# A hybrid diffusion layer on one core: the first tile's modulation in two halves, its shift used with the fifth tile, and the squares of the last four tiles in two calls

## The chip, the core and the metric

The kernel runs on one core of a Trainium2 chip. The time is that of one execution on the device in microseconds. Before the change it was 1232.01 us, the median of 3 runs (1231.84 to 1232.99).

Names used below: PE is the engine for matrix products (its weight loads are PEld), DVE the vector engine, ACT the engine for functions and copies, POOL the general engine, SP the engine that issues loads. Each engine works through its own queue in order and waits on counters of the others.

## The reference, cut to what matters

The layer works on 512 latent tokens and 256 context tokens of 1024 channels. The stage that the change touches is the first one:

```
mod = silu(c) @ w_mod + b_mod            # shift sh1 and scale sc1 are its first two parts
h_lat = rmsnorm(x, norm1_g) * (1 + sc1) + sh1
h_ctx = rmsnorm(ctx, norm1_g) * (1 + csc1) + csh1     # the same weights, from c_ctx
p_lat = h_lat @ w_in                     # its columns: z, xBC, dt, q, k, v, gates
```

All later work (two token mixers, their merge, and the gated feed-forward part) follows from `h_lat` and `h_ctx` and is the same in both kernels.

## The kernel before

Channels lie on the 128 partitions, so `x` is eight tiles of 128 channels by 512 tokens (`xs_`, printed as `xsb`). Products in float32 are made of three: a value is split into a high and a low part, and high by high, low by high and high by low are added.

The opening stage computes the modulation and, in the same stretch, the first five of sixteen gate column blocks (`w0`, 640 columns) into five PSUM banks `pg` (printed as `mis`). Its steps are named by a letter and a tile number j:

- **A**j (`mod_rows`): 8 matmuls of `silu(c)` with the two 512 KB pieces of `wm1` that hold the shift and scale columns of tile j, into columns 0 to 255 of the PSUM tile `pmod` (printed as `acc`); the first 4 need the first piece, the last 4 the second. Then ACT copies the row out (`tm`), and the 640 columns of `w0` are split (`w0h`, `w0l`).
- **B**j (`mod_cols`): two small matmuls turn the row into columns 256 to 259 of the same `pmod`; ACT makes of them the factor `a1` (first) and the shift `s1` (then; it is part of `s32`).
- **H**j (`prep`): for j below 4 (`NU`) the raw tile times `a1`, split into `ah` (ACT) and `al` (DVE), because the token norms are not known yet; for j from 4 on the normalised and shifted tile (`norm`: DVE makes the product, ACT `hlh`, DVE `hll`). **N**j is the same for the first four tiles, later.
- **P**j:ab (`products`): the three products of tile j into the banks a to b-1.
- **Z**j (`shifts`): the shift of tile j times `w0`, into `pbias`, since the first four tiles went in without their shift.
- **sq** (`squares`): ACT squares a tile, DVE adds it to `ssq`. **sum_l** (PE), a root on DVE and POOL, and **put_l** (PE) spread the token norms; ACT copies them to `r_l`; **scale_a/b** multiply the five banks by them on DVE.
- **hold**, **keep**: matmuls whose result nobody reads.

After the eight tiles follows the first of the large products (`gemm` of q), in whose middle the context's sum (`sum_c`, from `te`) and its spreading are done.

PE's order is fixed by the string `order` (the schedule is manual for PE). The queues of DVE, ACT and POOL are ordered by the framework's scheduler from the same calls, so they move when the calls move. SP issues loads in the order of the calls; it has eight completion counters in turn, so a load is issued only after the load eight places ahead of it has landed, and also when its buffer is free: `wm` has 6 buffers, `w0` has 4. A PSUM tile counts as one thing for these waits: a matmul into one part of `pmod` waits for the copies out of any other part that stand ahead of it in the calls.

Of the kernel before, what the change touches and what calls it, by code (L numbers as in the profile page):

```python
# [9 lines left out]
F32 = mybir.dt.float32  # L10
F32R = mybir.dt.float32r
U8 = mybir.dt.uint8
AF = mybir.ActivationFunctionType
# [5 lines left out]
P = 128  # L19
D = 1024  # L20
L = 512
LC = 256
KT = D // P
# [4 lines left out]
V_BMOD = 0  # L28
V_N1 = 48
# [15 lines left out]
def tile_hybrid_layer(  # L45
# [33 lines left out]
    V, S, G, T = nc.vector, nc.scalar, nc.gpsimd, nc.tensor  # L79
# [221 lines left out]
    NU, NG = 4, 5  # L301
    first = {}
    gates = []
    with tc.tile_pool(name="spool", bufs=1) as sp:
# [10 lines left out]
        def load_mod(i):  # L315
            t = sp.tile([P, 4, 256], F32, tag="wm", name="wm", bufs=6)
            nc.sync.dma_start(t, wm1[i].rearrange("p (k c) -> p k c", k=4))
            return t

        def load_w0(j):  # L320
            r = sp.tile([P, 640], F32, tag="w0", name="w0", bufs=4)
            nc.sync.dma_start(r, w0[j])
            return r

        def load_x(k):
            nc.sync.dma_start(xs_[:, 2 * k : 2 * k + 2, :], xT[k].rearrange("p (k t) -> p k t", k=2))
# [2 lines left out]
            nc.sync.dma_start(xs_[:, k, :], xT[k // 2, :, k % 2 * L : k % 2 * L + L])  # L329

        nc.sync.dma_start(ccs, cc)
        mod_raw = {i: load_mod(i) for i in range(2)}
        nc.sync.dma_start(ident, ident_d)
        nc.sync.dma_start(vec[:, :V_N2], vecs[:, :V_N2])
        w0_raw = {0: load_w0(0)}
# [4 lines left out]
        mod_raw.update({i: load_mod(i) for i in (4, 5)})  # L340
        w0_raw[2] = load_w0(2)
        load_x(1)
        load_x(2)
        load_x(3)
        mod_raw.update({i: load_mod(i) for i in (6, 7)})
        w0_raw[3] = load_w0(3)
        nc.sync.dma_start(vec[:, V_N2:], vecs[:, V_N2:])
        G.memset(raw(still), 1.0)
        G.memset(csil32, 0.0)
# [17 lines left out]
        def mod_rows(j):  # L367

            for u in range(2):
                i = 2 * j + u  # L370
                w = mod_raw.pop(i) if i in mod_raw else load_mod(i)
                for k in range(4):
                    z = slice(32 * k, 32 * k + 32)
                    T.matmul(pmod[z, 0:256], csil32[:, 4 * u + k, :], w[:, k, :], start=u == 0, stop=u == 1)
            row = tmp("tm")[:, :256]
            tc.keep_in_program_order(S.copy(row, pmod[:, 0:256]))
            if j + 1 < KT and j + 1 not in w0_raw:
                w0_raw[j + 1] = load_w0(j + 1)
            W[j] = split_w(j)
            return row  # L380

        def mod_cols(j, row):
            for i in range(2):
# [10 lines left out]
        def squares(x_, q, n, ks):  # L394
            for k in ks:
                sq = tmp(("ta", "tb")[k % 2])[:, :n] if k else q
                tc.keep_in_program_order(S.activation(sq, x_[:, k, :], AF.Square))
                if k:
                    V.tensor_tensor(q, q, sq, ALU.add)
# [17 lines left out]
        def products(j, w, h, gs=range(NG)):  # L417

            st, en = j == 0, j in (NU - 1, KT - 1)
            for a, b in ((0, 0), (0, 1), (1, 0)):  # L420
                for i in gs:
                    T.matmul(  # L422
                        pg[i], w[a][:, i * P : (i + 1) * P], h[b], start=st and a + b == 0, stop=en and a == 1,
                        skip_group_check=True,
                    )

        def shifts(j):

            for g in range(3):
                n = 256 if g < 2 else P  # L430
                T.matmul(
                    pbias[32 * g : 32 * g + 32, 0:n], s32[:, j, :], w0_raw[j][:, 256 * g : 256 * g + n],
                    start=j == 0, stop=j == NU - 1,
                )

        r, W, H = {}, {}, {}
# [16 lines left out]
        def hold(n):  # L453
            for _ in range(n):
                T.matmul(unread[:, :256], still[:, :P], still, start=True, stop=True)
# [21 lines left out]
        def load_next():  # L477
# [18 lines left out]
            "sq_0": lambda: squares(xs_, ssq, L, range(1)),  # L496
            "sq_1": lambda: squares(xs_, ssq, L, range(1, 2)),
            "sq_2": lambda: squares(xs_, ssq, L, range(2, 4)),
            "sq_3": lambda: squares(xs_, ssq, L, range(4, 8)),
            "hold": lambda: hold(18),  # L500
            "keep": lambda: hold(6),
            "sq_c": lambda: squares(xc_, cq, LC, range(4)),
            "sq_d": lambda: squares(xc_, cq, LC, range(4, 8)),
            "sum_l": lambda: sums("l", ssq, 4),
# [11 lines left out]


        order = """
            hold A0 keep B0 H0 sq_0 keep Z0 P0:02 A1 P0:23 B1 H1 sq_1 P0:35 A2 P1:02 B2 H2 sq_2 P1:25 Z1 P2:02 sq_3 A3 P2:23 B3 H3
            P2:35 sum_l Z2 P3:02 A4 put_l P3:23 B4 H4 P3:35 scale_a Z3 scale_b rows A5 half P4:02 B5 H5 cols P4:25 A6  # L520
            P5:02 B6 H6 P5:24 A7 ctx N0 P5:45 B7 H7 next P6:02 N1 P6:25 N2 P7:02 sq_c N3 P7:25 sq_d
        """
        with tc.manual_schedule(engines={mybir.EngineType.PE}):
# [1563 lines left out]
def pack(  # L2087
    x, c, ctx, c_ctx, w_mod, b_mod, norm1_g, norm2_g, w_in, ssd_conv_w, ssd_conv_b, ssd_dt_bias, ssd_a_log, ssd_d,
    ssd_norm_g, w_o_ssd, w_o_att, att_sink, w_out, w_up, ffn_conv_w, ffn_conv_b, w_down, final_g,
):  # L2090
    f = lambda a: np.asarray(a)
    x, c, ctx, c_ctx, w_mod, w_in = f(x), f(c), f(ctx), f(c_ctx), f(w_mod)[0], f(w_in)[0]
    w_o_ssd, w_o_att, w_out, w_up, w_down = f(w_o_ssd)[0], f(w_o_att)[0], f(w_out)[0], f(w_up)[0], f(w_down)[0]
    ca = np.ascontiguousarray
    z0, xbc0, dt0 = 0, 2048, 5120
    q0 = dt0 + 64
    k0, v0, g0 = q0 + 1024, q0 + 1280, q0 + 1536
    half = np.r_[0:16, 32:48, 16:32, 48:64]
    perm = lambda base, heads: np.concatenate([base + 64 * h + half for h in range(heads)])
    A = np.arange  # L2100
    d = {}
    d["xT"] = ca(x[0].T.reshape(4, 2, P, L).transpose(0, 2, 1, 3).reshape(4, P, 2 * L))
    d["ctxT"] = ca(ctx[0].T.reshape(2, 4, P, LC).transpose(0, 2, 1, 3).reshape(2, P, 4 * LC))
    d["cc"] = ca(np.stack([c[0], c_ctx], 1).reshape(KT, P, 2).transpose(1, 0, 2))
    cw, fw = f(ssd_conv_w)[0], f(ffn_conv_w)[0]
    d["vecs"] = ca(
        np.concatenate(
            [_per_channel(f(a)) for a in (b_mod[0], norm1_g[0], norm2_g[0], final_g, ssd_norm_g[0])]
            + [_per_channel(cw[i]) for i in range(3)]
            + [_per_channel(f(ssd_conv_b)[0])]  # L2110
            + [_per_channel(fw[i]) for i in range(3)]
            + [_per_channel(f(ffn_conv_b)[0])],
            axis=1,
        )
    )
    dta = np.stack([f(ssd_dt_bias)[0].reshape(64), f(ssd_a_log)[0].reshape(64)], 1).reshape(2, 1, 32, 2)
    d["dta"] = ca(np.repeat(dta, 2, axis=1).reshape(P, 2))
    d["bc"] = ca(np.concatenate([f(ssd_d)[0], f(att_sink)[0]]))
    d["wm1"] = ca(w_mod[:, :2048].reshape(2, 4, P, 2, KT, P).transpose(4, 0, 2, 1, 3, 5).reshape(16, P, 1024))
    d["wm2"] = ca(w_mod[:, 2048:].reshape(4, 2, P, 8, 512).transpose(3, 0, 2, 1, 4).reshape(8, 4, P, 1024))  # L2120
    d["wq"] = _cols(w_in, perm(q0, 16))
    d["wk"] = _cols(w_in, perm(k0, 4))
    vdt = ca(w_in[:, np.r_[v0:g0, dt0:q0]].reshape(KT, P, 320).transpose(1, 0, 2)).reshape(P, KT * 320)
    d["wv"] = ca(np.pad(vdt, ((0, 0), (0, 320))).reshape(P, 3, 960).transpose(1, 0, 2))
    d["w0"] = ca(w_in[:, g0 : g0 + 640].reshape(KT, P, 640))
    d["wx"] = _cols(w_in, A(xbc0, dt0))
    d["wz"] = _cols(w_in, A(z0, xbc0))
    d["wg"] = _cols(w_in, A(g0, g0 + 2048))
    d["woa"] = _cols(w_o_att, A(1024))
    d["wos"] = _cols(w_o_ssd, A(1024))  # L2130
    d["wout"] = _cols(w_out, A(1024))
    d["wup"] = _cols(w_up, A(2 * NFF * P))
    wd = np.pad(w_down.reshape(11, 2, P, 2, 512), ((0, 1), (0, 0), (0, 0), (0, 0), (0, 0)))
    d["wdn"] = ca(wd.reshape(6, 2, 2, P, 2, 512).transpose(2, 4, 0, 3, 1, 5).reshape(4, 6, P, 1024))
    d["ident_d"] = np.eye(P, dtype=np.float32)
    inv = (10000.0 ** (-np.arange(0, 32, 2, dtype=np.float32) / np.float32(32))).astype(np.float32)
    t = np.arange(L)
    ang = np.concatenate([(t // 64).astype(np.float32)[None] * inv[:, None], (t % 64).astype(np.float32)[None] * inv[:, None]])
    cos, sin = np.cos(ang).astype(np.float32), np.sin(ang).astype(np.float32)
    d["cos_d"] = ca(np.tile(cos, (4, 1)))  # L2140
    d["sin_d"] = ca(np.tile(np.concatenate([-sin, sin]), (2, 1)))
    qq, kk = np.arange(P)[:, None], np.arange(384)[None]
    win = np.where((kk >= qq) & (kk <= qq + 256), 0.0, -NEG).astype(np.float32)
    zero = np.zeros((P, 256), np.float32)
    d["win_d"] = np.concatenate([zero, win, zero], axis=1)
    d["sel_d"] = (np.arange(P)[:, None] > np.arange(P)[None]).astype(np.float32)
    d["bm"] = ca(f(b_mod)[0, 5120:6144].reshape(2, 512))
    d["fg"] = ca(f(final_g))
    return d
# [12 lines left out]
```

## Time and profile before

| | |
|---|---|
| time, median of 3 runs | 1232.01 us |
| the profiled execution, its own time | 1232.22 us |
| its span in the trace | 1230.4 us (1.8 us lie outside it) |
| ACT busy | 687.0 us (56%) |
| DVE busy | 914.1 us (74%) |
| POOL busy | 167.9 us (14%) |
| bytes moved | 224.65 MB, mean 183 GB/s |
| granted PE clock | 0.998 of full speed |

In the first 60 us the queue of SP moves 17.91 MB. "Busy" counts an instruction from start to end; the matmuls of PE overlap each other, and their ends are modelled. A row of a timeline gives the start, the duration, engine, line, operation, what it writes and reads, how many there are, and in brackets how long its engine was idle ahead of it and what ended that. One float32 matmul of the program stands as two in the trace. The chain of waits gives for each piece the time by which it moved the end.

### The profile page before, as it was taken

The numbers are of one execution on the slowest core, as the hardware profiler recorded it, in microseconds if no ns is written. First come the engines' busy times: TensorE is split into PE (matmuls) and PEld (weight loads), VectorE is DVE, ScalarE is ACT, GpSimd is POOL, SyncE is SP. The second block draws the span as 40 slices with busy tenths as digits, with TensorE's granted clock in tenths as the row PEclk, the third lists the DMA queues.
The fourth block names the chain that finished last, engine by engine and source line by source line (L and its number), as shares of the span: only waits on it lengthen the run. The fifth ranks groups of instructions, "written<-read, shape, count | busy, mean of one in ns | idle before, by whom it ended". The sixth has DMA issues, their size and how long they took to land.

```text
span 1230.4 us, 17460 instructions
## 1 busy us (share of the span) xinstructions
PE 1218.5 (99%) x6328; PEld 996.3 (81%) x6328; DVE 914.1 (74%) x1484; ACT 687.0 (56%) x1302; POOL 167.9 (14%) x174
## 2 busy tenths in 40 slices
PE   9999999999999999999999999999999999999997
PEld 6798888888878877777777778888988888888886
DVE  4757888888555698697886786677688788886566
ACT  4657787787443556566586572223544444444543
POOL 0000111121100033333351530000200000000000
PEclk9999999999999999999999999999999999999999
DMA  9652678877946235345347466776144444457785
GB/s 354 245 159 89 218 194 194 212 198 211 225 141 211 91 123 147 121 131 185 122 138 203 136 205 221 225 245 236 48 166 148 145 150 153 153 169 248 243 318 183
DMA packets 108630, 224.65 MB, mean 183 GB/s; under 512 B 9600, under 2 KB 48832, under 8 KB 108544
## 3 DMA queue, kind: packets, MB, share of 16 engines
q1 hardware_dynamic: 101056, 197.32, 48.9%
q0 software_dynamic: 6912, 25.17, 8.7%
q8 instruction: 50, 0.82, 0.3%
q10 hardware_dynamic: 576, 1.05, 0.2%
q14 instruction: 36, 0.29, 0.1%
HBM read 193.29 MB, written 49.87 MB: 198 GB/s over the span
## 4 chain that ended last, share of the span: by engine, by line
PE 92%; DVE 3%; DMA 2%; ACT 2%; issue 1%; SPq 0%; POOLq 0%; ACTq 0%; DVEq 0%
PE acc L197 19%; PE acc L200 19%; PE acc L198 19%; PE acc L1919 3%; PE acc L1917 3%; PE acc L1918 3%; PE score L811 3%; PE po L860 3%; PE pt L847 2%; PE mis L1480 2%; PE mis L1385 2%; DMA wm<-wm 1%; PE mis L422 1%; PE acc L930 1%; PE acc L931 1%; PE acc L932 1%
## 5 line engine op out<-in xcount | busy, mean ns | idle before, releaser
L197 PE MATMUL acc<-hlh,whi 128*128 128x512 f32 x488 | 199.3, 408 | 0.0
L150 DVE TENSOR_TENSOR wlo<-wraw,whi 128x1024 fp32r<-128x1024 f32 (+2 forms) x119 | 143.4, 1207 | 71.9 <-ACT whi L149 62.2
L149 ACT CAST whi<-wraw 128x1024 fp32r<-128x1024 f32 (+2 forms) x119 | 122.8, 1033 | 127.4 <-PE acc L198 75.0
L200 PE MATMUL acc<-hlh,wlo 128*128 128x512 f32 x488 | 191.4, 392 | 0.0
L198 PE MATMUL acc<-hll,whi 128*128 128x512 f32 x488 | 190.7, 391 | 0.0
L197 PE MATMUL acc<-mh,whi 128*128 128x512 f32 x360 | 141.0, 392 | 0.0
L200 PE MATMUL acc<-mh,wlo 128*128 128x512 f32 x360 | 140.1, 389 | 0.0
L198 PE MATMUL acc<-ml,whi 128*128 128x512 f32 x360 | 140.0, 389 | 0.0
L200 PEld LDWEIGHTS acc<-hlh,wlo 128*128 128x128 f32 x488 | 91.6, 188 | 20.3
L198 PEld LDWEIGHTS acc<-hll,whi 128*128 128x128 f32 x488 | 91.9, 188 | 17.5 <-issue 1.7
L197 PEld LDWEIGHTS acc<-hlh,whi 128*128 128x128 f32 x488 | 91.8, 188 | 17.5 <-issue 2.2
L198 PEld LDWEIGHTS acc<-ml,whi 128*128 128x128 f32 x360 | 67.6, 188 | 14.5 <-issue 0.5
L197 PEld LDWEIGHTS acc<-mh,whi 128*128 128x128 f32 x360 | 67.6, 188 | 14.3 <-issue 0.5
L200 PEld LDWEIGHTS acc<-mh,wlo 128*128 128x128 f32 x360 | 67.6, 188 | 14.2
L820 DVE CUSTOM_DVE_ANT_0 p<-score,winm,nsink 128x512 f32<-128x512 f32 (+1 forms) x64 | 51.9, 810 | 15.2 <-PE score L811 13.7
L1268 DVE SCALAR_TENSOR_TENSOR ta<-acc,half,ta 128x511 f32<-128x511 f32 (+1 forms) x66 | 43.8, 663 | 25.7 <-ACT ta L1267 25.6
L1267 ACT ACTIVATE ta<-acc,half 128x512 f32<-128x512 f32 (+1 forms) x66 | 46.7, 708 | 27.0 <-PE acc L200 25.7
L1275 ACT ACTIVATE tb<-ta 128x512 f32<-128x512 f32 (+1 forms) x44 | 23.5, 534 | 65.2 <-DVE ta L1269 59.2
L827 ACT ACTIVATE p<-p,mneg 128x512 f32<-128x512 f32 (+1 forms) x64 | 49.7, 777 | 15.3 <-DVE mneg L820 14.7
L1387 POOL TENSOR_TENSOR st<-st,eT 128x512 f32<-128x512 f32 x24 | 33.5, 1396 | 170.5 <-ACT st L1405 162.3
L197 PE MATMUL acc<-hch,whi 128*128 128x256 f32 x176 | 54.4, 309 | 0.0
L855 DVE TENSOR_TENSOR ptl<-pt,pth 128x512 fp32r<-128x512 f32 x72 | 47.5, 686 | 8.5 <-ACT pth L851 7.8
(503 smaller groups left out, 2970.1 us busy)
## 6 DMA issues: line engine op xcount, KB each, us to landing
wraw<-wup SPq DMA_DIRECT2D x44, 512.0 KB, 3.6
wt_d<-wdn POOLq DMA_DIRECT2D x36, 512.0 KB, 7.8
fb<-cs_d SPq DMA_DIRECT2D x32, 512.0 KB, 6.6
wraw<-wm SPq DMA_DIRECT2D x32, 512.0 KB, 4.1
wraw<-wx SPq DMA_DIRECT2D x24, 512.0 KB, 3.5
wraw<-wt_d SPq DMA_DIRECT2D x20, 512.0 KB, 4.0
sp_d<-te SPq DMA_DIRECT2D x33, 256.0 KB, 2.1
wm<-wm SPq DMA_DIRECT2D x16, 512.0 KB, 7.7
```

The costliest lines, as they stand in the source:

```text
L149: S.copy(hi[:, :n], r[:, :n])
L150: V.tensor_tensor(lo[:, :n], r[:, :n], raw(hi[:, :n]), ALU.subtract)
L197: T.matmul(ps, wh, xh[:, k0 + k, :], start=a, stop=False)
L198: T.matmul(ps, wh, xl[:, k0 + k, :], start=False, stop=False)
L200: T.matmul(ps, wl, xh[:, k0 + k, :], start=False, stop=b)
L811: T.matmul(ps[:, o : o + len(z) * P], Q[h][:, b * P : (b + 1) * P], k[:, j, z[0] * P : (z[-1] + 1) * P], start=v == 0 and o % 512 in (0, P ...
L820: V.tensor_tensor_reduce(p[:, :w], d["ps"][i][:, o0 : o0 + w], m, op0=ALU.add, op1=ALU.min, scale=1.0, scalar=nsink[:, h : h + 1], accum_o ...
L827: S.activation(p, p, AF.Exp, bias=d["mneg"][:, i : i + 1], scale=-1.0, accum_out=d["den"][:, i : i + 1])
L855: V.tensor_tensor(d["ptl"][x], d["pt"][x], raw(d["pth"][x]), ALU.subtract)
L860: T.matmul(d["po"], vst[:, cols[x], j, :], d[y][x], start=x == 0 and y == "pth", stop=x == c - 1 and y == "ptl")
L1267: S.activation(o[:, :n], ps[:, :n], AF.Identity, scale=hcol(base_w, stride + i), bias=hcol(base_b, i))
L1268: V.scalar_tensor_tensor(o[:, 1:n], ps[:, 0 : n - 1], hcol(base_w, i), o[:, 1:n], ALU.mult, ALU.add)
```

## The change

The first tile's two pieces of `wm1` are packed anew: piece 0 holds all scale columns of tile 0, piece 1 all its shift columns. Piece 0 is the first load; piece 1 goes behind all tiles of `x`. `A0` and `B0` are gone; `S0` and `a0` make the scale from piece 0 alone (8 matmuls of 128 columns, one small matmul, one activation), and `T0` and `s0` make the shift later, next to `A4` and `B4`, in other columns of the same `pmod`. `Z0` moves next to `Z3`, and the first `Z` to start `pbias` is now `Z1`. The pieces 6 and 7 of `wm1` and the `w0` of tile 3 are loaded ahead of the last four tiles of `x`, no longer behind them. The squares of tiles 4 to 7 are two calls, one ahead of tile 3's `H` and one behind it, and `sum_l` and `put_l` stand later. For tile 0 the product with `w0l` comes ahead of that with `al`. The twelve matmuls of the two `keep` become 3 and 8. `w0` has 7 buffers in place of 4.

```diff
-            r = sp.tile([P, 640], F32, tag="w0", name="w0", bufs=4)
+            r = sp.tile([P, 640], F32, tag="w0", name="w0", bufs=7)
...
-        mod_raw = {i: load_mod(i) for i in range(2)}
+        mod_raw = {0: load_mod(0)}
...
         load_x(1)
+        mod_raw.update({i: load_mod(i) for i in (6, 7)})
+        w0_raw[3] = load_w0(3)
         load_x(2)
         load_x(3)
-        mod_raw.update({i: load_mod(i) for i in (6, 7)})
-        w0_raw[3] = load_w0(3)
+        mod_raw[1] = load_mod(1)
         nc.sync.dma_start(vec[:, V_N2:], vecs[:, V_N2:])
...
+        def first_rows(i):
+            w = mod_raw.pop(i).rearrange("p k c -> p (k c)")
+            z0 = 0 if i == 0 else 3 * P
+            for u in range(2):
+                for k in range(4):
+                    z, c = slice(32 * k, 32 * k + 32), P * (4 * u + k)
+                    T.matmul(
+                        pmod[z, z0 : z0 + P], csil32[:, 4 * u + k, :], w[:, c : c + P], start=u == 0, stop=u == 1,
+                    )
+            row = tmp("tc")[:, :P]
+            tc.keep_in_program_order(S.copy(row, pmod[:, z0 : z0 + P]))
+            if i == 0:
+                W[0] = split_w(0)
+            return row
+
+        def first_cols(i, row):
+            c = 258 if i == 0 else 260
+            T.matmul(pmod[:, c : c + 2], row, sel2, start=True, stop=True)
+            if i == 0:
+                S.activation(a1[:, 0, :], pmod[:, c : c + 2], AF.Identity, scale=col(V_N1, 0), bias=bp1[:, 0:1])
+            else:
+                S.activation(s1[:, 0, :], pmod[:, c : c + 2], AF.Identity, bias=col(V_BMOD, 0))
...
-            for a, b in ((0, 0), (0, 1), (1, 0)):
+            for a, b in ((0, 0), (0, 1), (1, 0)) if j else ((0, 0), (1, 0), (0, 1)):
...
-                    start=j == 0, stop=j == NU - 1,
+                    start=j == 1, stop=j == NU - 1,
...
-            "sq_3": lambda: squares(xs_, ssq, L, range(4, 8)),
+            "sq_3": lambda: squares(xs_, ssq, L, range(4, 6)),
+            "sq_4": lambda: squares(xs_, ssq, L, range(6, 8)),
...
-            hold A0 keep B0 H0 sq_0 keep Z0 P0:02 A1 P0:23 B1 H1 sq_1 P0:35 A2 P1:02 B2 H2 sq_2 P1:25 Z1 P2:02 sq_3 A3 P2:23 B3 H3
-            P2:35 sum_l Z2 P3:02 A4 put_l P3:23 B4 H4 P3:35 scale_a Z3 scale_b rows A5 half P4:02 B5 H5 cols P4:25 A6
+            hold S0 keep_a a0 H0 sq_0 keep_b P0:02 A1 P0:23 B1 H1 sq_1 P0:35 A2 P1:02 B2 H2 sq_2 P1:25 Z1 P2:02 A3 sq_3 P2:23 B3 H3 sq_4
+            P2:35 Z2 P3:02 sum_l A4 T0 P3:23 B4 s0 put_l H4 P3:35 scale_a Z0 Z3 scale_b rows A5 half P4:02 B5 H5 cols P4:25 A6
...
+    for i in range(2):
+        d["wm1"][i] = wm[:, :, :, 1 - i, 0].transpose(2, 0, 1, 3).reshape(P, 1024)
```

Three places show what the engines' queues make of it. The first is PE's queue from the end of tile 2's products to A5, before. L241 is sum_l, L431 a Z, L422 products, L374 A4 and then A5, L258 put_l, L384 B4.

```order
L241 MATMUL acc<-rmsc,ssq 128x1 x4
L431 MATMUL acc<-w_143,s_117 32x256 x2
...
L374 MATMUL acc<-wm,csil_116 32x256 x8
L258 MATMUL acc<-ident,rs 128x128 x4
...
L384 MATMUL acc<-sel_119,tm 128x2 x2
...
L431 MATMUL acc<-w_152,s_117 32x256 x2
L431 MATMUL acc<-w_152,s_117 32x128
L374 MATMUL acc<-wm,csil_116 32x256 x8
```

The same stretch of PE's queue in the changed kernel, from the last product of tile 3's first two banks on. L375 is A4 (A5 in the last row), L390 is T0, L401 is s0, and L456 with `w_127` is Z0.

```order
L447 MATMUL mis<-ah,w0l 128x512 x2
L241 MATMUL acc<-rmsc,ssq 128x1 x4
L375 MATMUL acc<-wm,csil_116 32x256 x8
L390 MATMUL acc<-wm,csil_116 32x128 x8
...
L409 MATMUL acc<-sel_119,tm 128x2 x2
L401 MATMUL acc<-sel_119,tc 128x2
L258 MATMUL acc<-ident,rs 128x128 x4
...
L456 MATMUL acc<-w_127,s_117 32x256 x2
L456 MATMUL acc<-w_127,s_117 32x128
L456 MATMUL acc<-w_148,s_117 32x256 x2
...
L375 MATMUL acc<-wm,csil_116 32x256 x8
```

sum_l moved behind Z2 and P3:02, put_l behind B4, and T0, s0 and Z0 are new in this stretch. In the program the first matmul of T0 waits for ACT's copy of A4's row (`tm`), since both use `pmod`; s0 waits for ACT's second activation of B4, for the same reason.

The second place is ACT's queue around tile 3's factor, before. L397 is a square, L376 the copy of A3's row, L385 and L386 make `a1` and `s1`, L413 makes `ah`.

```order
L397 ACTIVATE ta<-xsb 128x512
L397 ACTIVATE tb<-xsb 128x512
L376 COPY tm<-acc 128x256
L149 CAST w0h<-w_152 128x640
L385 ACTIVATE a_87<-acc,bp_88,vec 128x2
L386 ACTIVATE s_117<-acc,vec 128x2
L413 ACTIVATE ah<-xsb,a_87 128x512
L149 CAST w0h<-w_350 128x640
```

The same place of ACT's queue in the changed kernel, where the squares are L422 and `ah` is L438.

```order
L149 CAST w0h<-w_148 128x640
L377 COPY tm<-acc 128x256
L410 ACTIVATE a_87<-acc,bp_88,vec 128x2
L411 ACTIVATE s_117<-acc,vec 128x2
L438 ACTIVATE ah<-xsb,a_87 128x512
L422 ACTIVATE ta<-xsb 128x512
L422 ACTIVATE tb<-xsb 128x512
L422 ACTIVATE ta<-xsb 128x512
L422 ACTIVATE tb<-xsb 128x512
```

The four squares of tiles 4 to 7 moved from ahead of A3's copy to behind tile 3's `ah`; on DVE their four additions stand behind tile 3's `al` accordingly.

The third place is DVE's queue at the end of the stage, before. L404 and L406 are the first and the last step of a norm (the last two L406 are tiles 3 and 7, in this order), L399 adds a context square, L150 with `wlo` splits the weights of q and of k.

```order
L404 SCALAR_TENSOR_TENSOR xsb<-xsb,a_87,r_l 128x512
L399 TENSOR_TENSOR te<-te,tb 128x256
L406 SCALAR_TENSOR_TENSOR hll<-xsb,s_117,hlh 128x512 x2
L399 TENSOR_TENSOR te<-te,ta 128x256
L399 TENSOR_TENSOR te<-te,tb 128x256
L150 TENSOR_TENSOR wlo<-wraw,whi 128x1024
```

The same place of DVE's queue in the changed kernel (L429 and L431 are the norm's steps, tile 7's L431 now ahead of tile 3's).

```order
L429 SCALAR_TENSOR_TENSOR xsb<-xsb,a_87,r_l 128x512
L150 TENSOR_TENSOR wlo<-wraw,whi 128x1024 x2
L431 SCALAR_TENSOR_TENSOR hll<-xsb,s_117,hlh 128x512
L507 CAST sel<-self__585 128x128
L424 TENSOR_TENSOR te<-te,ta 128x256
L431 SCALAR_TENSOR_TENSOR hll<-xsb,s_117,hlh 128x512
```

Both splits of q's and k's weights moved ahead of tile 7's last step. On ACT the two casts that they read moved likewise ahead of tile 7's `hlh`, with two context squares between them. Behind this stage no queue's order differs.

More of the change, by code (lines that the diff above doesn't have):

```diff
@@ L498, in tile_hybrid_layer @@
             "sq_2": lambda: squares(xs_, ssq, L, range(2, 4)),
-            "sq_3": lambda: squares(xs_, ssq, L, range(4, 8)),
+            "sq_3": lambda: squares(xs_, ssq, L, range(4, 6)),
+            "sq_4": lambda: squares(xs_, ssq, L, range(6, 8)),
             "hold": lambda: hold(18),
-            "keep": lambda: hold(6),
+            "keep_a": lambda: hold(3),
+            "keep_b": lambda: hold(8),
+            "S0": lambda: rows.update(s=first_rows(0)),
+            "T0": lambda: rows.update(t=first_rows(1)),
+            "a0": lambda: first_cols(0, rows.pop("s")),
+            "s0": lambda: first_cols(1, rows.pop("t")),
             "sq_c": lambda: squares(xc_, cq, LC, range(4)),
@@ L2118, in pack @@
     d["bc"] = ca(np.concatenate([f(ssd_d)[0], f(att_sink)[0]]))
-    d["wm1"] = ca(w_mod[:, :2048].reshape(2, 4, P, 2, KT, P).transpose(4, 0, 2, 1, 3, 5).reshape(16, P, 1024))
+    wm = w_mod[:, :2048].reshape(2, 4, P, 2, KT, P)
+    d["wm1"] = ca(wm.transpose(4, 0, 2, 1, 3, 5).reshape(16, P, 1024))
+    for i in range(2):
+        d["wm1"][i] = wm[:, :, :, 1 - i, 0].transpose(2, 0, 1, 3).reshape(P, 1024)
     d["wm2"] = ca(w_mod[:, 2048:].reshape(4, 2, P, 8, 512).transpose(3, 0, 2, 1, 4).reshape(8, 4, P, 1024))
```

## The prediction
> **What bounds the kernel.** I read the page first: its busy times, then its chain of work.
>
> ```profile
> PE 1218.5 (99%) x6328; PEld 996.3 (81%) x6328; DVE 914.1 (74%) x1484; ACT 687.0 (56%) x1302; POOL 167.9 (14%) x174
> PE 92%; DVE 3%; DMA 2%; ACT 2%; issue 1%; SPq 0%; POOLq 0%; ACTq 0%; DVEq 0%
> ```
>
> PE is the bound nearly everywhere, so what the opening stage gains or loses at its end is carried to the end of the program: no queue's order differs behind it. Second I read the chain of waits in the first 60 us.
>
> ```profile
> 13.37 10.55 DMA wm<-wm
> 23.97 0.64 PE acc L374 x8
> 24.61 0.90 PE mis L422 x3
> 25.51 0.34 PE acc L384 x4
> ...
> 27.34 0.79 PE acc L241 x8
> 28.13 0.56 PE acc L431 x4
> 28.69 1.57 PE mis L422 x6
> 30.26 1.00 PE acc L374 x16
> ...
> 32.88 1.50 PE mis L422 x6
> ...
> 35.80 1.62 PE mis L422 x6
> ```
>
> The reader is to see a border: up to 24 us the chain ends with loads (13.37, 10.55 us of it), the last of them the second piece of A3; from there it is PE's own work. The change takes loads away from the first part and puts PE work into the second. I call A3's end X; before it is 24.61.
>
> **The first part: what is gained.** The timeline gives the waits.
>
> ```profile
> 9.26 0.83 DVE L154 TENSOR_TENSOR w0l<-w,w0h 128x640 fp32r<-128x640 f32 x1
> 9.39 2.85 SPq L326 DMA_DIRECT2D xsb<-xT  x3
> 10.21 0.75 DVE L414 SCALAR_TENSOR_TENSOR al<-xsb,a,ah 128x512 fp32r<-128x512 f32 x1
> 10.23 0.73 PE L422 MATMUL mis<-ah,w0h 128*128 128x512 f32 x2
> 12.14 1.07 PE L374 MATMUL acc<-wm,csil 128*32 128x256 f32 x16
> 15.85 0.33 SPq L347 DMA_DIRECT2D vec<-vecs  x1
> 15.87 1.07 PE L374 MATMUL acc<-wm,csil 128*32 128x256 f32 x16
> 23.09 0.16 PEld L374 LDWEIGHTS acc<-wm,csil 128*32 128x32 f32 x8 [0.36 <-DMA wm<-wm]
> 13.20:24.00 10.80, 10.56 (x74) 6.99 (x73) 6.54 (x10) 7.87 (x17) 0.00 (x0) 1.00 1.03 414
> ```
>
> An issue of SP shows the landing of the load eight places ahead: tile 0 of x landed by 9.39, the second piece of A2 by 15.85. The last row is a stage of the trace; its first numbers are the length and PE's busy time, its last is GB/s. One piece of `wm1` is 524 KB, at 414 GB/s 1.26 us, and it leaves the place ahead of everything else. So tile 0 lands at about 8.13, and its first products start at 10.23 - 1.25 = 8.98. Six such products take 1.50 (32.88), a pair 0.5. The pair with `w0l` comes next, whose split ends at 10.09 - 1.26 = 8.83, then the pair with `al`, ready at 10.96 - 1.25 = 9.71: no wait is left between them, and A1 starts at 8.98 + 1.5 = 10.5, that is 1.65 earlier than 12.14. From A1 to A3 PE has hardly a gap (10.56 of 10.80 busy). A2's second half starts at 15.87 - 1.65 + 0.5 = 14.7, and its piece lands at 15.85 - 1.26 = 14.6: in time by 0.1 us only. A3's own waits (0.36, and again for its second piece until 23.97) go as well, because its pieces now stand ahead of 1 MB of x. So A3 starts at 23.09 - 1.65 = 21.45 and ends 1.07 later: **X = 22.5, 2.1 gained**. S0 needs one piece alone and is done ahead of tile 0's landing, which covers it; with that cover gone it would cost its whole 0.6 (below, as T0).
>
> **The second part: what is paid.** Everything from X on counts fully. Rows that price it:
>
> ```profile
> 12.14 0.59 PEld L374 LDWEIGHTS acc<-wm,csil 128*32 128x32 f32 x16 [0.36 <-issue]
> 20.05 0.75 DVE L414 SCALAR_TENSOR_TENSOR al<-xsb,a,ah 128x512 fp32r<-128x512 f32 x1 [1.19 <-ACT ah L413]
> 20.71 0.69 DVE L399 TENSOR_TENSOR ssq<-ssq,ta 128x512 f32<-128x512 f32 x1
> 21.50 0.69 DVE L399 TENSOR_TENSOR ssq<-ssq,tb 128x512 f32<-128x512 f32 x1
> 24.68 0.37 ACT L376 COPY tm<-acc 128x256 f32<-128x256 f32 x1 [1.54 <-PE acc L374]
> 26.14 0.25 ACT L386 ACTIVATE s<-acc,vec 128x2 f32<-128x2 f32 x1
> 26.28 0.72 ACT L413 ACTIVATE ah<-xsb,a 128x512 fp32r<-128x512 f32 x1
> ```
>
> - **sum_l waits for the late squares: +1.4.** Tile 3's `ah` ends at 27.00 = X + 2.39. In the changed queues the four squares stand behind it on ACT, and their additions behind `al` on DVE: `al` from X + 2.42, the first addition 0.66 later (20.05 to 20.71), three more at 0.79 each, the last one 0.69 long, which ends at X + 6.14. PE comes to sum_l after P2 (27.34 = X + 2.73), Z2 (0.56) and P3:02 (1.57), at X + 4.86. It stands still until X + 6.25; A4, T0, B4 and all else queue behind it. The loads are no part of this: the two last pairs of x tiles move back by 0.8 MB net, 2 us. The last landed at some 21.7 (20.4, see the rivals, and 1.26), so it will by 23.7, and its squares start at X + 3.4 = 25.9. Without that cover each further us would go to sum_l one for one.
> - **T0 waits for the copy of A4's row: +0.5.** The copy starts 0.07 behind A's end and takes 0.37, and a handover more.
> - **T0: +0.6.** Eight matmuls, 16 in the trace. The trace has none of half the width; 16 of full width take 1.00 (30.26), the upper bound, and their 16 weight loads, which stay, 0.59, the lower. I take 0.6, for with half the columns the loads are what is left to bind.
> - **s0 waits for B4's two activations: +0.6**, then its own matmul: **+0.17**, half of B's 0.34. Before, B's matmuls end at 25.85 (25.51 + 0.34) and its second activation at 26.39. put_l queues behind s0, and with it `r_l` and all the scaling.
> - **Z0 between P3 and Z3: +0.56**, the price of Z2. Before, it stood ahead of tile 0's first products, beside ACT's and DVE's work for them, and cost nothing.
>
> These six make 3.8. P4:02 begins at 35.80 = X + 11.2 before and at X + 15.0 = 37.5 after: **1.7 later**. The scaling by `r_l` does not take over: between put_l and P4:02 stand P3:35 (1.50), Z0 and all that ran from there (32.88 + 1.50 = 34.38) to 35.80, some 3.5 us of PE work.
>
> [...]
>
> **The end of the stage: +0.7.** Third, the timeline around tile 7.
>
> ```profile
> 48.00 0.41 ACT L397 ACTIVATE te<-xcb 128x256 f32<-128x256 f32 x1
> 49.23 1.33 ACT L405 ACTIVATE hlh<-xsb,s 128x512 fp32r<-128x512 f32 x2
> 50.77 1.03 ACT L149 CAST whi<-wraw 128x1024 fp32r<-128x1024 f32 x1
> 51.44 0.30 PEld L422 LDWEIGHTS mis<-hll,w0h 128*128 128x128 f32 x2 [0.30 <-DVE hll L406]
> 52.10 1.22 DVE L150 TENSOR_TENSOR wlo<-wraw,whi 128x1024 fp32r<-128x1024 f32 x1
> 56.40 0.58 PE L241 MATMUL acc<-rmsc,te 128*128 128x1 f32 x4 [0.27 <-DVE nsink L485]
> ```
>
> PE waited at 51.44 for tile 7's `hll`. After the change two casts of 1.03 stand ahead of its `hlh` on ACT, and two splits of 1.22 ahead of `hll` on DVE. On the old clock: casts at 48.0 and 49.6 (two context squares between), the second split 50.65 to 51.87, `hll` 51.8 to 52.55. P7 stands still for 1.1 more than before. Of this 0.4 comes back at sum_c, which waited (0.27 and the handover) and no longer does, since PE is now behind the context's additions.
>
> **The sum**: -2.1 + 3.8 + 0.7 = +2.4. Against the profiled execution's own 1232.22 (span 1230.4 and 1.8 around it) this is 1234.6; its time stands 0.2 above the median, so against the runs 1234.4. What costs nothing: the 7 buffers (a wait of SP goes, but no load of A5 to A7 was late in the chain), one matmul of `keep` less, piece 1 (it lands some 5 us ahead of T0).
>
> **The rivals.**
>
> ```profile
> SPq L322 <- PE acc L431: 4.0, 1, 4.0
> 17.94 2.81 SPq L317 DMA_DIRECT2D wm<-wm  x2
> 6.70 0.17 DVE L359 TENSOR_REDUCE sel<-ident 128x2 f32<-128x8 f32 x1 [3.41 <-DMA ident<-ident_d]
> ```
>
> *The gain is halved (slower).* If a load at the front lands late, by the 1.2 us seen once before, A2's second piece binds, X comes 1.1 later and the sum is +3.5: 1235.5. It decides from 14.7 us on for that piece. For it: SP's two issues from 17.94 on wait for the second and the third pair of x tiles, landed by 17.9 and 20.4, two spacings of a load for one load. [...]
>
> *The waits shrink (no change).* If PE meets sum_l later by delays of its own, or the handovers at T0 and s0 hide in the modelled ends, half of 1.4 + 0.5 + 0.6 + 0.7 goes: +0.8, 1232.8. Against it: each is an order in a queue.
>
> *Loads bind beyond 24 us (faster).* SP waited 4.0 us for a `w0` buffer and no longer does. If A5 to A7 had waited for that, up to 4.0 goes: -1.6, and with the waits shrunk too -3.2, 1228.8. Against it: the chain has no load there.
>
> *Tile 0 starts no earlier*, so that the first part gains nothing: +4.5, 1236.5. It needs `ident` for a0, which DVE had at 6.70 and would have at 5.45; the copy (0.37) and the activations (0.54, as B's) end well ahead of 8.13.
>
> **How the numbers follow.** The sum as worked 0.56, gain halved 0.16, waits shrunk 0.17, loads bind 0.07, no earlier start 0.04. The own range of the first is +1.5 to +3.3. 0.2%, about what a measurement of this kernel can tell from no change, is 2.46 us and cuts it: 0.31 of it within, 0.25 slower. So slower 0.25 + 0.16 + 0.04 = 0.45, within 0.31 + 0.17 = 0.48, faster 0.07. The range, 1231.8 to 1236.2, takes in the first three cases.
>
> **What would show it.** Right: A1 near 10.5, A3's end near 22.5 with no wait for a load; PE idle for over 1 us ahead of L241 with DVE's addition as the releaser; gaps ahead of L390 and L401 ended by ACT; P4:02 near 37.5; P7's weight load waiting for L431 by over 1 us. Wrong: sum_l without a wait, a load in the chain behind 24 us, or P4:02 ahead of 35.8.

## The result, and the profile after

The changed kernel is slower: 1239.49 us (median of 5, 1237.90 to 1240.32) against 1232.62 (median of 5, 1231.84 to 1233.97), ratio 1.0056 [1.0045, 1.0068]. The prediction was 1234.4 in a range of 1231.8 to 1236.2: the sign is right, the size is not. The profiled execution took 1240.24 us with a span of 1238.4. Of all executions below one, among late_sum's eleven, ran in a slow state (1740.36 us at a mean clock of 0.653) and is left out of that run's count, median and ratio.

First the chain of waits of the changed kernel in the stage that the change touches (start, length, engine, tile and line).

```profile
22.19 0.89 PE mis L447 x3
...
27.66 0.70 DVE ssq L424
28.36 0.14 issue
28.50 1.02 PE acc L241 x8
29.52 1.04 PE acc L375 x16
...
30.59 0.38 ACT tm L377
...
31.01 1.08 PE acc L390 x16
32.09 1.58 PE mis L447 x3
33.67 0.66 PE acc L409 x4
...
34.91 0.59 PE acc L401 x2
35.50 0.95 PE acc L258 x4
36.45 2.56 PE mis L447 x6
39.01 1.43 PE acc L456 x6
...
40.86 1.11 PE acc L375 x14
41.98 1.60 PE mis L447 x6
...
63.42 0.34 PE acc L241 x4
```

A3 ends at 22.19 (X, forecast 22.5, before 24.61): no load stands in the way, so the first part came as forecast. P4:02 begins at 41.98 (forecast 37.5, before 35.80). Between the two the same instructions are longer than they were: three products of P3 take 1.58 here and 0.89 at 22.19; B4's matmuls (L409) take 0.66, where B3's before took 0.34; the six that follow 2.56, before 1.50 (32.88 in the prediction's chain); only at 41.98 are six products 1.60 again. sum_c (L241) stands at 63.42, before at 56.40: 7.0 later.

The reason is in a column of the profile that the prediction did not look at beyond 24 us. The windows view, changed kernel (length; busy time of PE, PEld, DVE, ACT, POOL; PEclk, the clock granted to TensorE, which is PE, as a share of full speed; DMA share; GB/s):

```profile
28.00:30.00 2.00, 1.50 (x20) 1.35 (x24) 1.00 (x4) 0.00 (x0) 0.13 (x1) 1.00 1.02 414
30.00:32.00 2.00, 1.51 (x28) 0.63 (x20) 0.46 (x1) 0.37 (x1) 1.34 (x1) 0.75 0.96 313
32.00:36.00 4.00, 3.40 (x16) 3.01 (x13) 0.00 (x0) 1.03 (x4) 0.00 (x0) 0.50 1.02 395
36.00:41.00 5.00, 5.00 (x29) 3.04 (x31) 3.31 (x6) 2.01 (x4) 0.00 (x0) 0.50 1.02 415
41.00:42.00 1.00, 1.00 (x13) 0.40 (x5) 1.00 (x3) 0.35 (x2) 0.00 (x0) 0.88 1.00 380
42.00:44.00 2.00, 2.00 (x12) 1.73 (x12) 0.92 (x2) 0.42 (x2) 0.00 (x0) 1.00 1.04 402
```

PEclk is 1.00 until 30, falls to half within the window from 30 to 32 (0.75 is 1.0 us of it at half, so the fall is at 31.0: from 30.60 to 30.90 it is 1.00, from 31.00 to 31.10 0.50), and is back at 41.24 (0.88 is 0.24 us at half; from 41.10 to 41.20 it is 0.50, from 41.24 to 41.30 1.00): 10.2 us at half speed. The kernel before shows 1.00 in every window from 22 to 40. DMA keeps its rate in the slow windows (395 and 415 GB/s, 414 from 28 to 30), so it is not what became slow.

The stops of TensorE that the prediction named, in the timeline (the bracket is the idle time ahead and what ended it):

```profile
28.50 1.02 PE L241 MATMUL acc<-rmsc,ssq 128*128 128x1 f32 x8 [1.43 <-DVE ssq L424]
31.01 1.08 PE L390 MATMUL acc<-wm,csil 128*32 128x128 f32 x16 [0.49 <-ACT tm L377]
34.91 0.59 PE L401 MATMUL acc<-sel,tc 128*128 128x2 f32 x2 [0.59 <-ACT s L411]
57.43 0.73 PE L447 MATMUL mis<-hlh,w0h 128*128 128x512 f32 x2 [0.17 <-ACT hlh L430]
58.73 0.73 PE L447 MATMUL mis<-hll,w0h 128*128 128x512 f32 x2 [0.57 <-DVE hll L431]
58.73 0.30 PEld L447 LDWEIGHTS mis<-hll,w0h 128*128 128x128 f32 x2 [1.01 <-DVE hll L431]
```

All of them are there and as long as forecast (1.4, 0.5, 0.6). P7's products with tile 7's `hll` start 16.75 us behind P4:02 (58.73 - 41.98), before 15.65 (51.45 - 35.80): 1.1 later, as forecast.

### The profile page after: what moved, and what is told of

Read it like the earlier page. It is cut to its first block, busy times and chain, and to the rows that moved or that the text cites. A ratio compares the mean times of both kernels' runs of the same rounds, so it can differ in the third digit from the quotient of the medians.

```text
span 1238.4 us, 17494 instructions
## 1 busy us (share of the span) xinstructions
PE 1222.4 (99%) x6343; PEld 1000.4 (81%) x6343; DVE 914.3 (74%) x1484; ACT 687.3 (55%) x1303; POOL 168.2 (14%) x174
## 4 chain that ended last, share of the span: by engine, by line
PE 94%; DVE 3%; ACT 1%; issue 1%; POOL 0%; POOLq 0%; ACTq 0%; DVEq 0%
PE acc L197 19%; PE acc L200 19%; PE acc L198 19%; PE score L842 3%; PE po L891 3%; PE acc L1948 3%; PE acc L1950 3%; PE acc L1949 3%; PE pt L878 2%; PE mis L447 2%; PE mis L1511 2%; PE mis L1416 1%; PE acc L961 1%; PE acc L962 1%; PE acc L963 1%; PE mis L1434 1%
## 5 line engine op out<-in xcount | busy, mean ns | idle before, releaser
L197 PE MATMUL acc<-hlh,whi 128*128 128x512 f32 x488 | 199.3, 408 | 0.0
L150 DVE TENSOR_TENSOR wlo<-wraw,whi 128x1024 fp32r<-128x1024 f32 (+2 forms) x119 | 143.5, 1207 | 69.5 <-ACT whi L149 60.1
L197 PE MATMUL acc<-mh,whi 128*128 128x512 f32 x360 | 141.0, 392 | 0.0
L197 PEld LDWEIGHTS acc<-hlh,whi 128*128 128x128 f32 x488 | 91.8, 188 | 17.6 <-issue 2.2
L197 PEld LDWEIGHTS acc<-mh,whi 128*128 128x128 f32 x360 | 67.6, 188 | 14.5 <-issue 0.5
L197 PE MATMUL acc<-hch,whi 128*128 128x256 f32 x176 | 54.4, 309 | 0.0
```

What stands on the lines that cost most here:

```text
L150: V.tensor_tensor(lo[:, :n], r[:, :n], raw(hi[:, :n]), ALU.subtract)
L197: T.matmul(ps, wh, xh[:, k0 + k, :], start=a, stop=False)
```

## The experiments

The theory: a stop of TensorE costs more than its length, because the granted clock falls behind it; the stop at sum_l is the one that does it. The rival: the waits and the added instructions themselves cost the 7 us, and the clock is a side show. The table has each run's longest stop of TensorE between 24 and 36 us in its profiled execution, the stretch from X to P4:02, the executions whose mean clock over the whole run was 0.996 or less (none of 68 executions of the kernel before was), median and ratio to the kernel before on the same chip. The count is a lower bound: 3.4 us at half clock, as in late_sum's profile, lower the mean over 1236 us by 0.0014 only, and the kernel before itself lies between 0.997 and 0.999.

| run | longest stop, us | X | X to P4:02, us | low clock | median, us | ratio [95%] |
|---|---|---|---|---|---|---|
| before | none over 0.1 | 24.61 | 11.19 | 0 of 68 | 1232 | 1 |
| after | 1.43 | 22.19 | 19.79 | 5 of 5 | 1239.49 | 1.0056 [1.0045, 1.0068] |
| after_again | 1.43 | 22.49 | 18.21 | 3 of 5 | 1238.77 | 1.0049 [1.0035, 1.0063] |
| before_split | 2.79 | 24.01 | 17.03 | 4 of 5 | 1238.27 | 1.0045 [1.0032, 1.0057] |
| fill_stall | 0.85 | 22.93 | 15.40 | 5 of 11 | 1235.36 | 1.0028 [1.0019, 1.0037] |
| no_stops | 0.98 | 23.16 | 13.87 | 5 of 11 | 1235.67 | 1.0024 [1.0015, 1.0033] |
| late_sum | 0.60 | 23.28 | 15.18 | 3 of 10 | 1234.8 | 1.0018 [1.0009, 1.0027] |
| fill_more | 0.60 | 22.57 | 15.45 | 1 of 8 | 1235.77 | 1.0027 [1.0017, 1.0037] |
| half_alone | 0.60 | 22.73 | 13.74 | 1 of 11 | 1234.71 | 1.0021 [1.0012, 1.0030] |
| stop_free | 0.38 | 22.31 | 13.91 | 0 of 11 | 1233.39 | 1.0008 [0.9999, 1.0017] |
| loads_alone | 0.29 | 23.40 | 12.95 | 0 of 11 | 1232.89 | 1.0008 [1.0000, 1.0017] |

**Filling the stop: fill_stall, fill_more, after_again.** The edit to the changed kernel (fill_stall with 5 in place of 8):

```diff
             "keep_b": lambda: hold(8),
+            "keep_c": lambda: hold(8),
...
-            P2:35 Z2 P3:02 sum_l A4 T0 P3:23 B4 s0 put_l H4 P3:35 scale_a Z0 Z3 scale_b rows A5 half P4:02 B5 H5 cols P4:25 A6
+            P2:35 Z2 P3:02 keep_c sum_l A4 T0 P3:23 B4 s0 put_l H4 P3:35 scale_a Z0 Z3 scale_b rows A5 half P4:02 B5 H5 cols P4:25 A6
```

> The changed kernel with five more of the matmuls that only keep TensorE busy (0.23 us each, 1.2 us in all) ahead of sum_l, where it stands still for 1.43 us; no result uses them, and every wait, load and real instruction stays. Theory (the stop lets the granted clock fall to half from 30 to 41 us, which makes the work there some 4.5 us longer): the clock stays at 1.00, the pair of products that takes 0.63 in that stretch takes 0.40, and the time falls from 1239.5 to about 1235.0. Rival one (the loss is the waits and added instructions themselves): the place behind sum_l does not move, 1239.5 or 0.2 more. Rival two (the fall comes from T0's 0.49 us wait and the sparse matmuls there, not from the stop at sum_l): the clock falls all the same, 1239.5.

> The changed kernel with eight of the matmuls that only keep TensorE busy ahead of sum_l (1.87 us) in place of fill_stall's five (1.2), which left 0.8 of the stop; every wait for data stays, T0's 0.49 too, and sum_l is itself held up by some 0.4. Theory (a long stop alone makes the clock fall): 1.00 in all windows of the profile, 0.997 and more in nearly every execution, where fill_stall had this in 6 of 11; time 1232 + 2.8 (fill_stall's executions at 0.998, 1234.75 in the middle, against 1231.95) + 0.4 = 1235.2, without the spread up to 1239. Rival (what falls is decided by T0, s0 and the sparse work around them): as many slow-clock executions as fill_stall or as the changed kernel, 1236 to 1239.5.

> The changed kernel itself, on this chip and beside the same executions of the kernel before, so that fill_more is compared with it directly. Both theories: 1239.5, clock 0.993 to 0.994 in every execution. Should some executions reach 0.998, the theory gives them about 1236 (1239.5 less some 4 us of slow clock).

The fillers take 0.12 us each here, not the 0.23 of those at the program's start that the expectations counted with: five shorten the stop from 1.43 to 0.85, eight to 0.49. So sum_l was not held up in either, and nothing differs from the changed kernel but what TensorE does in the idle time ahead of it. The chain of fill_more:

```profile
22.57 0.90 PE mis L447 x3
...
28.89 1.02 PE acc L241 x8
...
31.41 0.65 PE acc L390 x16
32.05 0.91 PE mis L447 x3
...
34.77 1.40 PE mis L447 x6
...
38.02 1.59 PE mis L447 x6
```

Its windows from 30 to 36 us:

```profile
30.00:32.00 2.00, 1.51 (x33) 0.66 (x26) 0.86 (x2) 0.37 (x1) 1.47 (x1) 1.00 0.88 308
32.00:36.00 4.00, 3.40 (x23) 2.73 (x19) 0.57 (x1) 1.87 (x6) 0.00 (x0) 1.00 0.93 334
```

sum_l starts 28.89 - 22.57 = 6.32 behind X, in the changed kernel 28.50 - 22.19 = 6.31: the data come just as late. PE is busy just as long in both stretches (1.51 and 3.40, as in the changed kernel's rows above). Yet the clock stays at 1.00, three products take 0.91 and not 1.58, and P4:02 begins 15.45 behind X and not 19.79. **These 4.34 us, the difference of two executions, are the clock:** piece by piece it is TensorE's own work from T0 to A5 that is longer, while the waits are the same (0.49 at T0 in both, 0.59 and 0.60 at s0). fill_stall gives 15.40. Its own eleven executions of one program say the same: six at a mean clock of 0.998 or 0.999 took 1234.37 to 1235.36, four at 0.996 took 1236.28 to 1236.94, one at 0.994 took 1239.24. (In no_stops and late_sum the groups overlap.) The changed kernel beside fill_more on one chip had 1238.77 against 1235.77, 3.0 more. Its profiled execution here fell for a shorter time:

```profile
30.00:32.00 2.00, 1.51 (x32) 0.77 (x24) 0.76 (x2) 0.37 (x1) 1.47 (x1) 0.87 0.81 325
...
38.00:40.00 2.00, 2.00 (x27) 1.23 (x28) 1.42 (x4) 1.45 (x3) 0.00 (x0) 0.93 1.02 414
```

That is from 31.48 (0.87) to 38.28 (0.93), 6.8 us, and P4:02 stands 18.21 behind X: 2.8 more than with the stop filled. Two of the five executions reached a mean clock of 0.998, at 1237.4, not at the expected 1236: the mean over a whole run also holds a fall at the program's end, where TensorE has no work (in the kernel before 0.50 from 1226 us on), and does not tell a short fall in the opening from none.

**The stop put into the kernel before: before_split.**

```diff
-            "sq_3": lambda: squares(xs_, ssq, L, range(4, 8)),
+            "sq_3": lambda: squares(xs_, ssq, L, range(4, 6)),
+            "sq_4": lambda: squares(xs_, ssq, L, range(6, 8)),
...
-            hold A0 keep B0 H0 sq_0 keep Z0 P0:02 A1 P0:23 B1 H1 sq_1 P0:35 A2 P1:02 B2 H2 sq_2 P1:25 Z1 P2:02 sq_3 A3 P2:23 B3 H3
+            hold A0 keep B0 H0 sq_0 keep Z0 P0:02 A1 P0:23 B1 H1 sq_1 P0:35 A2 P1:02 B2 H2 sq_2 P1:25 Z1 P2:02 A3 sq_3 P2:23 B3 H3 sq_4
```

> The kernel before with one part of the change alone: the squares divided into two pairs, the first behind A3, the second behind H3; loads, first tile and sum_l's place stay as before. Then the last square is added some 1.8 us after TensorE comes to sum_l. Theory (clock): a stop of 1.8 at sum_l, the clock at half for some 10 us behind it (4.5 us), and the casts of q and k ahead of tile 7 (0.7): 1232.6 + 7.0 = 1239.6. Rival (stops cost their own length): 1232.6 + 1.8 + 0.7 = 1235.1.

Its stop, and the two windows in which the clock falls and comes back:

```profile
29.50 1.84 PE L241 MATMUL acc<-rmsc,ssq 128*128 128x1 f32 x8 [2.79 <-DVE ssq L399]
```

```profile
28.00:30.00 2.00, 0.50 (x3) 0.53 (x3) 1.90 (x3) 0.74 (x2) 0.00 (x0) 0.74 0.62 251
...
34.00:36.00 2.00, 2.00 (x15) 0.88 (x18) 0.00 (x0) 0.00 (x0) 0.00 (x0) 0.55 0.97 352
```

The divided squares alone (with A3 ahead of the first pair), every load and the first tile as before, cost 6.3 us (1238.27 against 1231.95), nearly all that the whole change costs. The stop is 2.79, one us longer than expected, and the clock is at half from 28.96 to 35.80. By its length alone a stop of 2.79 would give 1231.95 + 2.8 + 0.7 = 1235.4, so the rival falls short by 2.8. In the trace P4:02 stands 5.84 further behind X than before (17.03 - 11.19), 3.05 more than the stop.

**Taking the stops out: late_sum, no_stops, stop_free.** The order from P2:35 to Z3 in the changed kernel, and below it in late_sum, no_stops and stop_free, in this order; all else is the changed kernel:

```diff
-P2:35 Z2 P3:02 sum_l A4 T0 P3:23 B4 s0 put_l H4 P3:35 scale_a Z0 Z3
+P2:35 Z2 P3:02 A4 P3:23 T0 sum_l B4 s0 put_l H4 P3:35 scale_a Z0 Z3
+P2:35 Z2 P3:02 A4 P3:23 T0 sum_l B4 put_l H4 P3:34 s0 P3:45 scale_a Z0 Z3
+P2:35 Z2 P3:02 A4 P3:23 sum_l T0 B4 P3:34 s0 put_l P3:45 H4 scale_a Z0 Z3
```

> The changed kernel with sum_l and T0 moved behind P3's last products, so that the squares are added up by the time and the row of A4 is copied; all the work stays. Theory (clock): both stops go, 1.43 + 0.49, and with them the fall of the clock, 4.5: about 1233.1, clock 1.00 in all windows of the stage. Rival (waits and work alone): only the 1.9 of the two stops go, about 1237.6.

> As late_sum, and also s0 behind the first half of P3's remaining products, so that it no longer waits for B4's two activations (0.6) and put_l does not queue behind it. Theory (clock): 0.6 less than late_sum, 1232.5, level with the kernel before. Rival (waits and work alone): 1237.6 - 0.6 = 1237.0.

> The changed kernel with sum_l behind A4 and P3's first products, T0 behind sum_l, and put_l between the halves of P3's remaining products, so that neither the squares, nor the copy of A4's row, nor POOL's power is waited for. Theory (only stops slow the clock): no stop above 0.5 from 20 to 44 us, clock 0.998 and more in every execution, and the time 1231.95 + 0.3 (P4's first products, from no_stops' 37.03 without its 0.92 of waiting for POOL, against 35.80) + 1.2 (the casts ahead of tile 7) = 1233.4. Rival (the clock falls in some executions whatever the stops): half of the executions at 0.996 as in no_stops, and a median near 1235.

late_sum and no_stops gain 3 to 5 us against the changed kernel's two medians, where waits alone were to give 1.9 and 2.5, but both miss the theory's numbers by 1.7 and 3.2. In no_stops put_l now waits 0.98 for POOL's power, since sum_l is late: a stop of the size that it was to remove, and 5 of its 11 executions show a low clock. In late_sum 0.60 ahead of s0 was enough in the profiled execution:

```profile
32.00:34.00 2.00, 1.40 (x8) 1.27 (x8) 0.00 (x0) 0.77 (x3) 0.98 (x1) 0.80 1.04 420
34.00:36.00 2.00, 2.00 (x7) 1.49 (x5) 1.31 (x3) 0.81 (x2) 0.00 (x0) 0.50 1.00 402
36.00:38.00 2.00, 2.00 (x28) 1.03 (x28) 1.42 (x4) 1.46 (x4) 0.00 (x0) 0.85 1.03 420
```

stop_free has no stop above 0.38, no window of its profile from 22 to 62 us and none of its 11 executions shows a low clock, and it came at the expected time (1233.39, expected 1233.4). It does all the work of the changed kernel, and the end of the stage is level with the kernel before, for the reason its chain shows:

```profile
36.22 1.20 PE mis L447 x4
...
56.35 0.58 PE acc L241 x4
```

A3 ends 2.30 earlier (22.31), and P4:02 is 0.42 later than in the kernel before (36.22 against 35.80): T0, s0, Z0 and the chain from put_l over `r_l` to tile 4's `hll` take back what the earlier start gave. sum_c is where it was (56.35, before 56.40). So that the time fits is luck: the expectation had 0.3 at P4:02 and 1.2 from the casts ahead of tile 7, none of which is left at sum_c. What stop_free's median has over the kernel before (1.1) arises in the last 20 us of the program, by the shift described in the next section.

**One part at a time: half_alone, loads_alone.** half_alone is the changed kernel with

```diff
-        mod_raw.update({i: load_mod(i) for i in (6, 7)})
-        w0_raw[3] = load_w0(3)
         load_x(2)
         load_x(3)
+        mod_raw.update({i: load_mod(i) for i in (6, 7)})
+        w0_raw[3] = load_w0(3)
...
-P2:02 A3 sq_3 P2:23 B3 H3 sq_4 P2:35 Z2 P3:02 sum_l A4 T0
+P2:02 sq_3 A3 P2:23 B3 H3 P2:35 sum_l Z2 P3:02 A4 T0
```

with the squares undivided (of the order only the stretch that differs is shown); loads_alone is the kernel before with the opposite swap of the loads, the divided squares, and sum_l and put_l as in stop_free.

> The first tile's scale half alone: S0, a0, T0, s0, Z0 and the seven buffers stay as changed, but the pairs of x tiles 2 and 3 are loaded ahead of the pieces of A3 again, the four squares are undivided ahead of A3, and sum_l stands where it stood before. Against the kernel before: one piece less ahead of all loads, -1.26; T0's wait for the copy, 0.5, T0 0.57 (measured in late_sum), s0's wait and matmul 0.77, Z0 0.56, the casts ahead of tile 7's hlh 0.7: +1.8 over 1231.95, 1233.8. Theory (the divided squares, by the stop at sum_l, make the large loss): 1233.8, up to 1235 where the two stops of half a microsecond that are left slow the clock in some executions. Rival (the first tile's part makes it): above 1237.

> The kernel before with the load order of the change (the pieces of A3 ahead of the pairs of x tiles 2 and 3) and its divided squares, but tile 0 and its modulation as before (no S0, T0, s0, late Z0), and with sum_l, put_l where stop_free has them, so that no stop arises. A3's waits for its loads (0.36 and the one for its second piece) go: 0.6 earlier, paid by nothing on TensorE. Theory: 1231.4 where TensorE sets the end of the stage; where the context's additions on DVE set it, as in stop_free (sum_c at 56.35 against 56.40), no change, 1232. Rival (the load order itself costs, by the squares or by the casts of q and k): 1233.5 or more.

half_alone is 2.4 us over the kernel before (1234.71 against 1232.27; expected 1.8). Without the late sum there is no stop over 0.6, and 1 of 11 executions has a low clock. loads_alone ends A3 1.21 earlier than before, twice what was expected, and is 0.8 over the kernel before all the same, at the edge of what can be told (expected: up to 0.6 faster, or no change): TensorE waits 0.7 for tile 7's `hll` at the end of the stage. So neither the first tile's half nor the load order makes the large loss, though the first costs 2.4 of it; each gives an earlier X, and neither turns it into time.

**The shift still later: late_shift, late_all.** late_shift is half_alone and late_all stop_free, each with T0, s0, Z0, rows and cols taken out of the two lines of the order ahead of this one, and Z0 as the last of the shifts. In both, N0 uses tile 0's shift before s0 has written it, so their output lacks that shift.

```diff
-            P5:02 B6 H6 P5:24 A7 ctx N0 P5:45 B7 H7 next P6:02 N1 P6:25 N2 P7:02 sq_c N3 P7:25 sq_d
+            P5:02 B6 H6 P5:24 A7 ctx N0 P5:45 B7 H7 next P6:02 N1 T0 P6:25 N2 s0 P7:02 sq_c Z0 rows N3 P7:25 cols sq_d
```

> half_alone with T0, s0 and Z0, and the rows and columns of the shift, moved behind P6, where TensorE waits for tile 7's split (only the last tanh needs them). Theory: -1.26 from the loads, +0.57 for T0 and 0.17 for s0, Z0 half covered by the wait at P7, 0.3: 1231.95 - 0.2 = 1231.7, level with the kernel before, clock 0.998. Rival (work of that size costs the same wherever it stands, and the stop only moves): 1233.8 as half_alone.

> The changed kernel's loads and divided squares, sum_l and put_l as in stop_free, and T0, s0, Z0, rows and columns of the shift behind P6 as in late_shift. Theory: stop_free's 1233.4 less T0, s0 and Z0 where they lie in the wait at P7 (about 1.2 of them): 1232.2. Rival (P7's wait is DVE's and ACT's work, which the moved pieces lengthen): 1233.4 or above.

Both came out slower than expected: 1239.30 (ratio 1.0059 [1.0046, 1.0071]) and 1235.35 (1.0027 [1.0016, 1.0038]). The clock stays at 1.00 in the windows from 24 to 62 us. The list of TensorE's waits in late_shift:

```profile
PE acc L241 <- DVE te L424: 1.2, 1, 1.2
PE acc L197 <- ACT whi L149: 1.2, 1, 1.2
```

The copies of rows and columns now stand in ACT's queue ahead of the context's last squares, and sum_c waits for these (1.2, before 0.3). In late_shift sum_c still stands only 0.5 later than before (56.90); most of its 7 us arise behind it. A later large product (L197) waits 1.2 for the cast of its weights and v's first one (L723, from 72.9 us on) 0.7, and behind the stop at L723 the clock falls once more, in an execution whose mean is 0.997:

```profile
72.00:74.00 2.00, 1.32 (x5) 1.02 (x5) 2.00 (x4) 1.62 (x3) 0.00 (x0) 0.81 0.44 78
74.00:76.00 2.00, 2.00 (x6) 1.52 (x6) 2.00 (x4) 0.62 (x1) 0.00 (x0) 0.50 0.79 263
76.00:78.00 2.00, 2.00 (x9) 1.62 (x8) 0.01 (x1) 0.00 (x0) 0.00 (x0) 0.84 0.82 181
```

That is from 73.24 to 76.64. The end of the stage is bound by ACT and DVE as much as by TensorE: work of TensorE that passes through ACT is not free there. That is the mechanism of late_all's rival, and these two orders gain nothing.

## Why the prediction was wrong, step by step

- *"What is gained"* was right. X came 2.42 earlier (forecast 2.1). S0 was covered only just: tile 0 of x was there by 7.79, the scale's own activation (7.41 to 7.77) ended last, and the first products started at 8.57 (forecast 8.98). In late_sum's and no_stops' profiles X came 1.0 to 1.1 later than in the changed kernel's (23.28 and 23.16): A1 took 1.27 and 1.29 from its start to the next product, in the changed kernel's 1.00, and TensorE stood 0.22 and 0.41 until the second piece of A2 had landed. What the rival "the gain is halved" describes happens in single executions, here in two of eight profiles of kernels with both the scale half and the new load order.
- *"sum_l waits for the late squares: +1.4"* was right as a wait (1.43), so were T0's 0.5 (0.49) and s0's 0.6 (0.59). T0's own 0.6 was right at full clock: 0.57 in late_sum's chain (below), 0.65 in fill_more's (above). The 1.08 in the changed kernel's profile is T0 at the clock of 0.50, from 31.00 on.

```profile
30.05 0.57 PE acc L390 x16
```

- *"These six make 3.8"* is 15.45 - 11.19 = 4.26 with the clock at 1.00 (fill_more): 0.4 too small, s0's matmul among it (0.38, taken as 0.17) and sum_l's own, which take 1.02 behind the stop (0.79 before).
- *"The end of the stage: +0.7"* was right: from P4:02 to sum_c 63.42 - 41.98 = 21.44, before 56.40 - 35.80 = 20.60, so 0.84.
- **The step that failed is the second part, "what is paid"**: it priced every instruction behind the stop by rows of the kernel before, where the clock is 1.00, and every stop by its length. The missing term is 4.34 us in the profiled execution, 2.8 in the second one. The list of what would make the prediction wrong did not name it, though the windows that it quoted have the column. By these terms sum_c's move of 7.02 is divided as -2.42 + 4.26 + 4.34 + 0.84. With the clock at 1.00 (fill_more) sum_c stands 3.05 later than before and the median is 3.7 over the kernel before: inside the range.
- *"Carried to the end of the program"* holds to 1217 us and not for the last 20. The last transposes of the output in the two chains, and the last sum of the final norm:

```profile
1216.53 0.44 PE acc L1957 x4
...
1224.69 0.23 DVE ms L1975
```

```profile
1222.89 0.44 PE acc L1988 x4
...
1232.76 0.23 DVE ms L2006
```

The shift is 6.36 and then 8.07. ACT waits there for pieces of `wt_d`, from 1205 us on 3.9 in all, but 2.8 in the kernel before too. Between the same two places the shift grows by 1.7 to 2.1 in after, after_again, fill_more and stop_free, by 1.6 in late_all, by 1.3 in half_alone, and by 0.3 at most in before_split, fill_stall, late_sum, no_stops, loads_alone and late_shift, of which four have the changed first tile too. So it does not follow from the change's parts as they were tried; what sets it is open. The executions of the kernel before lie 3.8 us apart (1230.89 to 1234.64), so it may be its spread as well.

## What to carry to other kernels

When a change makes TensorE stand still, price the work behind the stop as well as the stop (here 4.34 us behind one of 1.43): look at the granted clock by windows, and if a stop can't be ordered away, fill it with matmuls that nobody reads (eight of them were worth 3 us here). A transfer made earlier pays only if the consumers behind it keep up: here the wait for the late additions of squares (0.7 us each on DVE) took 1.4 of the 2.4 us that the earlier loads had won, and the clock behind it up to 4 more. And work moved off the start of a stage that waited for loads into one that is bound by TensorE is not saved but paid for: stop_free is that account without the stops, and it comes out level.

## What the hardware showed that was not expected

- **The falls in five profiles lasted near one, two or three times 3.4 us.** 31.00 to 41.24 in the changed kernel (10.24), 31.48 to 38.28 in its second profile (6.80), 28.96 to 35.80 in before_split (6.84), 33.20 to 36.60 in late_sum and 73.24 to 76.64 in late_shift (3.40): three, two, two, one and one times 3.4, each 3.4 us at half worth some 1.4 us here (4.34 / 3, 2.76 / 2). What sets these lengths was not shown. The same kernel falls in some executions and not in others: fill_stall had a mean clock of 0.996 or less in 5 of 11, after_again 0.994 in three and 0.998 in two.
- **A stop of 0.60 us was enough in one profile, and the clock stayed low with TensorE busy.** The changed kernel, with stops of 1.43 and 0.49 us ahead of the fall in both its profiles, had a low clock in at least 8 of 10 executions; late_sum, with one of 0.60 in its profile, in at least 4 of 10 (3 at 0.996 or less, and the profiled one at 0.997). From 36 to 41 us in the changed kernel the clock is 0.50 with PE at 5.00 busy of 5.00. What makes the clock fall, beside the length of a stop, was not settled: this stretch has sums of one column, 32-column weights and transposes, and fill_more, with stops of 0.49, 0.49 and 0.60 in a row, kept a mean of 0.997 or more in 7 of 8 executions.
